# Second FFN: weights asked for behind a product's bank reads, a weight sum made with its own unit, the last down weights in the raw buffers

## The chip, the cores and the metric

The kernel runs on one core of a Trainium2 chip. The metric is the device time of one execution in microseconds. The time before is the median of three runs.

## What is computed

Two layers of a hybrid backbone over 512 latent and 256 context tokens, width 1024. Each layer is a mixer and then a gated FFN with a convolution over tokens; in the second layer only the latent tokens are needed. The change touches the second layer's FFN, with `z` of 512 x 1024, an up projection to 2 x 2816 and a down projection back to 1024:

```python
def conv_ffn(z, w_up, conv_w, conv_b, w_down):
    h = z @ w_up
    t = h.shape[1]
    half = CONV_W // 2
    hp = jnp.pad(h, ((0, 0), (half, half), (0, 0)))
    h = sum(hp[:, i:i + t] * conv_w[i] for i in range(CONV_W)) + conv_b
    a, g = jnp.split(h, 2, axis=-1)
    return (jax.nn.silu(g) * a) @ w_down
...
        hl = hl + mod_l[5] * conv_ffn(modulate(rms_norm(hl, norm2_g[layer]), mod_l[3], mod_l[4]),
                                      ffn_up[layer], ffn_conv_w[layer], ffn_conv_b[layer], ffn_down[layer])
...
    return rms_norm(hl, final_g)
```

## The kernel before

Each factor of a product is split into a high part (rounded to the matmul's type) and a low part (what is left), and one product is three matmuls: high by high, high by low, low by high. The FFN of the second layer is `layer1_end`; it runs from about 1216 us of the profile to the end.

**The up projection.** The 2816 features are 22 tiles of 128, p = 0 to 21. A tile stands for a gate tile and a value tile, so p has weights of 1024 x 256. For p = 0 and 1 it is made by plain block products ("C", `classical`). For p = 2 to 21 it is made by seven Strassen products ("S", `strassen`) over two halves of features and tokens. Each product is twelve matmuls of 128x256 (`product`, lines 1398 to 1400 in turn: high by high, high by low, low by high; the low half of the weights is read by line 1400 alone). P1, P6, P7 and P4 of one p accumulate into one PSUM bank, which ACT copies out after each (lines 1463, 1466, 1475, 1479); the next product into that bank waits for the copy. P5, P2 and P3 go to a second bank and are added by DVE (lines 1472, 1476, 1484). After P3(p), `finish(p)` makes the convolution (ACT line 1420 twice, DVE line 1422 four times), the Silu (ACT, line 1426), the product (DVE, line 1428) and the split into high and low (ACT line 131, DVE line 132). The order on TensorE, from one tile to the next, is P3(p-1), P6(p), P5(p), P2(p), P7(p), P1(p+1), P4(p), P3(p).

**The down projection** runs in eight chunks of features (3, 3, 3, 3, 3, 2, 2, 3 tiles). A step ("D") is three matmuls of 128x512; the steps of a chunk are woven between the products of later tiles, so that a D or two stand between most products. DVE adds a finished output tile to the stream (line 1498). The last chunk ("E") comes after the last product.

**Weight units.** `prepare` makes one unit: the factor of one product, or of one or two down steps. Its high half is a cast on ACT (line 1297). Its low half is either a subtraction on DVE (line 1303; A11, A12, S2 and down weights) or a negation on ACT (line 1300) and a DMA that POOL issues and that adds the source onto it (line 1301; S1, S3, S4, A22, and all of the first tiles). The product that takes the unit needs the DMA landed. S1 to S4 are sums of weight blocks, made on DVE (line 1318); all four are made when the tile's first unit, A11, is prepared. P1 takes A11, P2 A12, P3 S4, P4 A22, P5 S1, P6 S2 and P7 S3.

**What sets the order.** TensorE's order is written by hand in `events`. The other engines' instructions are ordered by the scheduler, which follows the order in which the code emits them and the waits it foresees. `weights(e)` asks for units up to five (`ASK`) ahead of the event's own in the order of use, and does so before the event's product is emitted. ACT, DVE and POOL each work in order, and so does SP, which issues the loads. Buffers are rings: 11 weight tiles (`WT`), 4 raw tiles of 1024 columns for up weights (`RAWS`), 2 raw tiles of 512 for down weights (`rawd`).

Of the kernel before, what the change touches and what calls it, by code (L numbers as in the profile page):

```python
# [10 lines left out]
F32 = mybir.dt.float32  # L11
F32R = mybir.dt.float32r
AF = mybir.ActivationFunctionType
ALU = mybir.AluOpType
# [22 lines left out]
PLAIN = 2  # L37
ASK = 5
# [3 lines left out]
def hybrid_backbone_kernel(ctx: ExitStack, tc: tile.TileContext, A: dict, out: bass.AP):  # L42
    nc = tc.nc
    pe, act, dve, pool = nc.tensor, nc.scalar, nc.vector, nc.gpsimd
# [3 lines left out]
    wp = ctx.enter_context(tc.tile_pool(name="wp", bufs=1))  # L48
# [3 lines left out]
    def nm(s):  # L52
        uid[0] += 1
        return f"{s}_{uid[0]}"

    def slab(dt=F32):
        return sb.tile([128, TW], dt, tag="slab", name=nm("sl"), bufs=SLAB)

    def half(dt=F32):
        return sb.tile([128, 512], dt, tag="half", name=nm("hf"), bufs=HALVES)  # L60
# [10 lines left out]
    def one():  # L71
        return pp.tile([128, 512], F32, tag="one", name=nm("on"), bufs=4)
# [4 lines left out]
    def bc(ap):  # L77
        return ap.bitcast(F32)
# [30 lines left out]
    def raw_tile(n):  # L109
        return wp.tile([128, n], F32, tag="raw", name=nm("raw"), bufs=RAWS, padded_shape=[128, 1024])  # L110

    def wtile(n=1024):
        return wp.tile([128, n], F32R, tag="w", name=nm("w"), bufs=WT, padded_shape=[128, 1024])
# [938 lines left out]
    for t in range(6):  # L1052
# [4 lines left out]
        if t < 4:  # L1057
            raw = half()
# [12 lines left out]
    for t in range(4):  # L1071
        raw = half()
# [169 lines left out]
    def layer1_end(x3, yds):  # L1242
# [8 lines left out]
        ch = CHUNKS[1]  # L1251
# [11 lines left out]
        for c in range(len(ch) - 1):  # L1263
# [3 lines left out]
            n = len(steps) - keep  # L1267
# [13 lines left out]
        def per(c):  # L1281
            return 2 if ch[c] <= 2 else 1

        def key(e):
            if e[0] == "C":
                return ("A", e[1], e[3])
            if e[0] == "S":
                return ("A", e[1], src_of[e[2]])
            return ("D", e[1], e[2] // per(e[1]))
# [3 lines left out]
        raws, sums, units = {}, {}, {}  # L1293
        asked = [0]

        def lows(h, l, src, by_dma):
            act.copy(out=h, in_=src)
            if by_dma:

                act.activation(out=l, in_=src, func=AF.Identity, scale=-1.0)  # L1300
                pool.dma_start(out=l, in_=src, accum_op=ALU.add)
            else:
                dve.tensor_tensor(out=l, in0=src, in1=bc(h), op=ALU.subtract)

        def prepare(k):
            if k[0] == "A":
                _, p, n = k
                if p not in raws:
                    rg, ra = raw_tile(1024), raw_tile(1024)
                    nc.sync.dma_start(out=rg, in_=A["ffn_up_w"][1, NF + p])  # L1310
                    nc.sync.dma_start(out=ra, in_=A["ffn_up_w"][1, p])
                    t = {"A11": rg[:, 0:512], "A12": rg[:, 512:1024], "A21": ra[:, 0:512], "A22": ra[:, 512:1024]}
                    raws[p] = t
                    if p >= PLAIN:
                        for o, x, y, op in (("S1", "A21", "A22", ALU.add), ("S2", "S1", "A11", ALU.subtract),
                                            ("S4", "A12", "S2", ALU.subtract), ("S3", "A11", "A21", ALU.subtract)):
                            t[o] = slab()[:, 0:512]
                            dve.tensor_tensor(out=t[o], in0=t[x], in1=t[y], op=op)
                w = wtile()
                h, l = w[:, 0:512], w[:, 512:1024]  # L1320
                lows(h, l, raws[p].pop(n), n in ("S1", "S3", "S4", "A22") or p < PLAIN + 2)
            else:
                _, c, u = k
                n, f0, w = per(c), ends[c] - ch[c], ch[c] * 128
                raw = wp.tile([128, 512], F32, tag="rawd", name=nm("rawd"), bufs=2)[:, :n * w]
                nc.sync.dma_start(out=raw.rearrange("p (m c) -> p m c", m=n),
                                  in_=A["ffn_down_w"][1, u * n:u * n + n, :, f0 * 128:f0 * 128 + w].rearrange(
                                      "m p c -> p m c"))
                t = wtile()
                h, l = t[:, 0:n * w], t[:, 512:512 + n * w]  # L1330
                lows(h, l, raw, False)
            return h, l

        def weights(e, ahead=ASK):
            i = seq.index(key(e))
            while asked[0] < min(len(seq), i + 1 + ahead):
                units[seq[asked[0]]] = prepare(seq[asked[0]])
                asked[0] += 1
            return units[seq[i]]
# [110 lines left out]

        def strassen(p, n):
            w = weights(("S", p, n))
            if n == "P1":
                zb[p] = one()[:, 0:256]
                hidden(p)
            if n == "P5":
                t = two()
                xy[p] = (t[:, 0:256], t[:, 512:768])
            hg, ha = hs[p]
            z = zb.get(p)  # L1460
            if n == "P1":
                product(z, w, B["B11"], True, False)
                act.copy(out=hg[:, H0], in_=z)  # L1463
            elif n == "P6":
                product(z, w, B["T2"], False, False)
                act.copy(out=hg[:, H1], in_=z)
            elif n == "P5":
                product(xy[p][0], w, B["T1"], True, False)
            elif n == "P2":
                y = xy[p][1]  # L1470
                product(y, w, B["B21"])
                dve.tensor_tensor(out=hg[:, H0], in0=y, in1=hg[:, H0], op=ALU.add)
            elif n == "P7":
                product(z, w, B["T3"], False, False)
                act.copy(out=ha[:, H1], in_=z)
                dve.tensor_tensor(out=ha[:, H1], in0=xy[p][0], in1=ha[:, H1], op=ALU.add)
            elif n == "P4":
                product(z, w, B["T4"], False, True)
                act.copy(out=ha[:, H0], in_=z)
                del zb[p]  # L1480
            else:
                x = xy.pop(p)[0]
                product(x, w, B["B22"], False, True)
                dve.tensor_tensor(out=hg[:, H1], in0=x, in1=hg[:, H1], op=ALU.add)
                finish(p)
# [3 lines left out]
        def down(e, a=0, b=512):  # L1489
            c, m, i = e[1:4]  # L1490
            h, l = weights(e)
            if i == 0:
                acc[0] = (two() if e[0] == "E" and a else one())[:, 0:b - a]
            o = (m % per(c)) * ch[c] * 128 + i * 128
            uh, ul = us[ends[c] - ch[c] + i]
            mm3(acc[0], (h[:, o:o + 128], l[:, o:o + 128]), (uh[:, a:b], ul[:, a:b]), i == 0, i == ch[c] - 1)
            if i == ch[c] - 1:
                dve.scalar_tensor_tensor(out=x3[:, m, a:b], in0=acc[0], scalar=modT[1][:, 0, 40 + m:41 + m],
                                         in1=x3[:, m, a:b], op0=ALU.mult, op1=ALU.add)
                if m == KT - 1 and (e[0] == "D" or a):  # L1500
                    for f in range(ends[c] - ch[c], ends[c]):
                        del us[f]
# [41 lines left out]
        with tc.manual_schedule(engines={mybir.EngineType.PE}):  # L1544
            for m in range(KT):
                part(0, m)
            for m in range(KT):
                part(1, m)
                if m == 2:
                    rows[0][1]()  # L1550
                if m == 4:
                    normed(0, rows[0][2]())
            yds.clear()
            for n, e in enumerate(events):
                if e[0] == "C":
                    classical(*e[1:])
                    if n == 0:
                        rows[1][1]()
                    if n == 2:
                        rb = rows[1][2]()  # L1560
                    if n == 4:
                        normed(1, rb)
                        differences()
                elif e[0] == "S":
                    strassen(*e[1:])
                elif e[0] == "D":
                    down(e)
                else:
                    _, _, m, i, gi = e
                    down(e, *GH[gi][:2])  # L1570
                    if i < ch[-1] - 1:
                        continue
                    final[gi][0]((m,))
                    if gi == 1 and m == 2:
                        final[0][1]()
                    if gi == 1 and m == 4:
                        normed_out(0)
            final[1][1]()
            normed_out(1)

    layer1_end(x3, yds)


# [111 lines left out]
```

## Time and profile before

| | |
|---|---|
| median of 3 runs | 1602.92 us (1601.92 to 1606.02) |
| the profiled execution: its time | 1602.01 us |
| the profiled execution: its span | 1600.2 us |
| TensorE busy | 1539.1 us, 96% of the span |
| DVE, ACT, POOL busy | 69%, 50%, 22% |
| chain of work that ended last | TensorE 86%, DVE 5%, ACT 3%, DMA 2% |

The span is what the profiler saw between the first and the last instruction; the 1.8 us around it belong to the execution's time. TensorE carries the chain. Idle time of the other engines costs nothing unless TensorE waits for them, so the table by stretches and TensorE's own waits are the views to read, and after them the timeline of the engine that each wait names.

### The profile page before, as it was taken

The page shows a single profiled execution, that of the slowest core. Times are in us where ns is not written, and L with a number is a line of the kernel's source. Part 1 is how long each engine was busy: PE and PEld are TensorE (multiplying, and loading weights), DVE is VectorE, ACT ScalarE, POOL GpSimd, SP SyncE. Part 2 cuts the span into 40 slices and gives each one's busy share as a digit, 9 for nine tenths or more (in the row PEclk, how much of TensorE's full clock was granted, in tenths as well). Part 3 has the DMA queues.
Part 4 walks back from the last instruction along what each step waited for, and adds up shares of the span by engine and source line. Part 5 has one row for each costly group of instructions (what it writes and reads, how often), then busy time and mean ns, then how long its engine had stood idle before and what let it go on. Part 6 is the DMA issues. An engine that isn't in the chain of part 4 may idle for free.

```text
span 1600.2 us, 25191 instructions
## 1 busy us (share of the span) xinstructions
PE 1539.1 (96%) x9394; PEld 1290.4 (81%) x9394; DVE 1106.6 (69%) x1955; ACT 806.1 (50%) x1574; POOL 353.0 (22%) x607
## 2 busy tenths in 40 slices
PE   6998999999999999999999999999999799999996
PEld 3786666658888888888888888778779799999986
DVE  4667765575469967865487557866667788877775
ACT  4447876674334233232331324535666767766663
POOL 0146444440011011010100100122324222222213
PEclk9999999999999999999999999999999899999998
DMA  9410014354123523622254211321134677776651
GB/s 314 158 53 27 1 53 159 106 172 164 54 80 112 158 66 122 208 65 66 66 172 145 63 57 45 108 66 40 40 87 99 146 181 172 165 175 161 167 119 65
DMA packets 81068, 179.19 MB, mean 112 GB/s; under 512 B 9393, under 2 KB 23729, under 8 KB 80945
## 3 DMA queue, kind: packets, MB, share of 16 engines
q1 hardware_dynamic: 67408, 152.93, 30.4%
q0 software_dynamic: 13536, 24.65, 9.0%
q8 instruction: 74, 1.21, 0.3%
q14 instruction: 50, 0.40, 0.1%
HBM read 150.80 MB, written 2.10 MB: 96 GB/s over the span
## 4 chain that ended last, share of the span: by engine, by line
PE 86%; DVE 5%; ACT 3%; issue 2%; DMA 2%; POOL 1%; SPq 0%; DVEq 0%; ACTq 0%; POOLq 0%
PE tw L125 9%; PE tw L126 9%; PE tw L127 9%; PE on L125 8%; PE on L126 7%; PE on L127 7%; PE on L621 3%; PE on L613 2%; PE on L1398 2%; PE on L1399 2%; PE on L1400 2%; PE tw L298 2%; PE tw L295 2%; PE tw L297 2%; PE tw L1398 2%
## 5 line engine op out<-in xcount | busy, mean ns | idle before, releaser
L125 PE MATMUL tw<-sl,w 128*128 128x512 f32 (+1 forms) x832 | 281.9, 339 | 0.1
L126 PE MATMUL tw<-sl,w 128*128 128x512 f32 (+1 forms) x832 | 280.9, 338 | 0.0
L127 PE MATMUL tw<-sl,w 128*128 128x512 f32 (+1 forms) x832 | 280.3, 337 | 0.0
L120 DVE TENSOR_TENSOR w<-raw,w 128x1024 fp32r<-128x1024 f32 (+3 forms) x119 | 137.7, 1159 | 139.8 <-PE tw L126 98.9
L119 ACT CAST w<-raw 128x1024 fp32r<-128x1024 f32 (+3 forms) x119 | 117.4, 990 | 175.3 <-PE tw L127 152.7
L125 PEld LDWEIGHTS tw<-sl,w 128*128 128x128 f32 x832 | 157.1, 189 | 27.4 <-issue 3.6
L125 PE MATMUL on<-sl,w 128*128 128x512 f32 (+2 forms) x504 | 174.0, 346 | 0.0
L126 PEld LDWEIGHTS tw<-sl,w 128*128 128x128 f32 x832 | 157.1, 189 | 18.9 <-issue 0.8
L127 PE MATMUL on<-sl,w 128*128 128x512 f32 (+2 forms) x504 | 171.7, 341 | 0.0
L126 PE MATMUL on<-sl,w 128*128 128x512 f32 (+2 forms) x504 | 171.7, 341 | 0.0
L127 PEld LDWEIGHTS tw<-sl,w 128*128 128x128 f32 x832 | 156.8, 188 | 17.7
L945 POOL TENSOR_SCALAR sm<-sm,csum,cw 128x2 f32<-128x2 f32 x44 | 30.3, 690 | 477.4 <-ACT sm L944 477.4
L1398 PE MATMUL on<-sl,w 128*128 128x256 f32 x384 | 109.8, 286 | 11.0 <-ACT sl L1463 9.9
L572 POOL TENSOR_SCALAR sl<-sl,sm 128x768 f32<-128x768 f32 (+2 forms) x96 | 84.7, 883 | 159.8 <-DVE sm L571 137.6
L125 PEld LDWEIGHTS on<-sl,w 128*128 128x128 f32 x504 | 95.6, 190 | 19.3 <-issue 7.3
L1399 PE MATMUL on<-sl,w 128*128 128x256 f32 x384 | 109.3, 285 | 0.0
L1400 PE MATMUL on<-sl,w 128*128 128x256 f32 x384 | 109.1, 284 | 0.0
L127 PEld LDWEIGHTS on<-sl,w 128*128 128x128 f32 x504 | 95.3, 189 | 11.1
L126 PEld LDWEIGHTS on<-sl,w 128*128 128x128 f32 x504 | 95.7, 190 | 9.8 <-DVE sl L132 0.2
L963 DVE SCALAR_TENSOR_TENSOR sl<-sl,cw,sl 128x770 f32<-128x770 f32 x88 | 89.4, 1019 | 19.6 <-ACT sl L960 17.9
L570 ACT ACTIVATE sl<-tw,sm 128x768 f32<-128x768 f32 (+2 forms) x96 | 81.8, 852 | 40.2 <-DVE sm L569 32.9
L569 DVE TENSOR_REDUCE sm<-tw 128x1 f32<-128x768 f32 (+2 forms) x96 | 84.9, 886 | 18.2 <-PE tw L787 12.0
(318 smaller groups left out, 3829.0 us busy)
## 6 DMA issues: line engine op xcount, KB each, us to landing
raw<-in_ffn_up_w_dram SPq DMA_DIRECT2D x88, 512.0 KB, 3.7
mraw<-in_mod_w_dram SPq DMA_DIRECT2D x96, 256.0 KB, 3.6
raw<-in_mod_w_dram SPq DMA_DIRECT2D x32, 512.0 KB, 4.0
w<-sl POOLq DMA_DIRECT2D x62, 256.0 KB, 4.1
rawd<-in_ffn_down_w_dram SPq DMA_DIRECT2D x48, 192.0 KB, 3.6
sl<-in_mod_w_dram SPq DMA_DIRECT2D x32, 256.0 KB, 5.4
raw<-in_ffn_down_w_dram SPq DMA_DIRECT2D x16, 512.0 KB, 3.6
w<-raw POOLq DMA_DIRECT2D x32, 256.0 KB, 4.4
```

The source lines that it names most:

```text
L119: act.copy(out=h, in_=raw)
L120: dve.tensor_tensor(out=l, in0=raw, in1=bc(h), op=ALU.subtract)
L125: pe.matmul(out=ps, lhsT=lh, rhs=rh, start=first, stop=False)
L126: pe.matmul(out=ps, lhsT=lh, rhs=rl, start=False, stop=False)
L127: pe.matmul(out=ps, lhsT=ll, rhs=rh, start=False, stop=last)
L569: dve.tensor_reduce(out=st[:, 0:1], in_=ps, axis=AX.X, op=ALU.max, negate=True)
L570: act.activation(out=p, in_=ps, func=AF.Exp, bias=st[:, 0:1], accum_out=st[:, 1:2])
L572: pool.tensor_scalar(out=p, in0=p, scalar1=st[:, 2:3], scalar2=1.0, op0=ALU.mult, op1=ALU.mult)
L963: dve.scalar_tensor_tensor(out=r[:, 2:end], in0=h[:, 2 + o:end + o], scalar=cw[:, f, t:t + 1], in1=r[:, 2:end], op0=ALU.mult, op1=ALU.add)
L1398: pe.matmul(out=ps, lhsT=h[:, o], rhs=rh, start=(first and k == 0), stop=False, skip_group_check=True)
L1399: pe.matmul(out=ps, lhsT=h[:, o], rhs=rl, start=False, stop=False, skip_group_check=True)
L1400: pe.matmul(out=ps, lhsT=l[:, o], rhs=rh, start=False, stop=(last and k == 3), skip_group_check=True)
```

## The change

Three edits in `layer1_end`:

1. `weights(e)` before a product or a down step asks for nothing ahead of the unit that it needs. The request for the five units ahead is made again, as `weights(e, ASK)`, after the product, its bank reads and, for P3, the `finish` have been emitted. (`classical` gives its own count ahead and keeps it.)
2. The four weight sums of a tile are no longer made at its first unit. Each is made in `part_of` when its own unit is prepared, S1 with S2. The raw tiles are held until the last of them, S4, is made.
3. The down weights of the last chunk are loaded into the ring of raw tiles (4 of them) instead of `rawd` (2).

TensorE's order is the same before and after.

```diff
+        def part_of(p, n):
+            t = raws[p]
+            if n not in t:
+                x, y, op = {"S1": ("A21", "A22", ALU.add), "S2": ("S1", "A11", ALU.subtract),
+                            "S4": ("A12", "S2", ALU.subtract), "S3": ("A11", "A21", ALU.subtract)}[n]
+                x, y = part_of(p, x), part_of(p, y)
+                t[n] = slab()[:, 0:512]
+                dve.tensor_tensor(out=t[n], in0=x, in1=y, op=op)
+            return t[n]
+
         def prepare(k):
             if k[0] == "A":
                 _, p, n = k
...
                     raws[p] = t
-                    if p >= PLAIN:
-                        for o, x, y, op in (("S1", "A21", "A22", ALU.add), ("S2", "S1", "A11", ALU.subtract),
-                                            ("S4", "A12", "S2", ALU.subtract), ("S3", "A11", "A21", ALU.subtract)):
-                            t[o] = slab()[:, 0:512]
-                            dve.tensor_tensor(out=t[o], in0=t[x], in1=t[y], op=op)
                 w = wtile()
                 h, l = w[:, 0:512], w[:, 512:1024]
-                lows(h, l, raws[p].pop(n), n in ("S1", "S3", "S4", "A22") or p < PLAIN + 2)
+                lows(h, l, part_of(p, n), n in ("S1", "S3", "S4", "A22") or p < PLAIN + 2)
             else:
                 _, c, u = k
                 n, f0, w = per(c), ends[c] - ch[c], ch[c] * 128
-                raw = wp.tile([128, 512], F32, tag="rawd", name=nm("rawd"), bufs=2)[:, :n * w]
+                if c < len(ch) - 1:
+                    raw = wp.tile([128, 512], F32, tag="rawd", name=nm("rawd"), bufs=2)[:, :n * w]
+                else:
+                    raw = raw_tile(n * w)
...
-        def weights(e, ahead=ASK):
+        def weights(e, ahead=0):
...
                 elif e[0] == "S":
                     strassen(*e[1:])
+                    weights(e, ASK)
                 elif e[0] == "D":
                     down(e)
+                    weights(e, ASK)
                 else:
                     _, _, m, i, gi = e
                     down(e, *GH[gi][:2])
+                    weights(e, ASK)
```

In the rows below, `w_...` is a weight tile, `sl_...` a working tile, `raw_...` a loaded up weight, `rawd_...` a loaded down weight, `on_...` a PSUM bank. In the changed kernel lines 1420, 1426, 1428, 1463, 1466, 1475 and 1479 have become 1428, 1434, 1436, 1471, 1474, 1483 and 1487; the sum's line 1318 is now 1312.

ACT around the copy of the first Strassen product, P1(2), before. The cast of `w_2271_12401` is that of a weight sum of p = 2:

```order
L1426 ACTIVATE sl_2252_12311<-sl_2252_12311 128x512
L131 ACTIVATE hf_2249_12256<-sl_2248_12251 128x512
L1297 CAST w_2271_12401<-sl_2261_12339 128x512
L1300 ACTIVATE w_2271_12401<-sl_2261_12339 128x512
L131 ACTIVATE hf_2254_12321<-sl_2253_12316 128x512
L1463 COPY sl_2266_12350<-on_2265_12349 128x256
```

ACT at the same place, after:

```order
L1428 ACTIVATE sl_2251_12312<-sl_2243_12186,cw_2126_11561 128x512
L1434 ACTIVATE sl_2250_12307<-sl_2250_12307 128x512
L131 ACTIVATE hf_2247_12252<-sl_2246_12247 128x512
L1471 COPY sl_2255_12322<-on_2254_12321 128x256
L1297 CAST w_2258_12343<-sl_2259_12344 128x512
L1300 ACTIVATE w_2258_12343<-sl_2259_12344 128x512
```

The copy (line 1463, now 1471) has moved ahead of the weight cast and of the second tile's high part; it stands directly behind the first tile's high part (line 131).

ACT from the cast of S3(6) to `finish(5)`, before. `w_2369_13064` is the unit S3(6), which P7(6) takes; `w_2381_13125` is A22(6) and `w_2382_13142` S4(6); lines 1475 and 1479 are the copies of P7(5) and P4(5), line 1463 that of P1(6):

```order
L1297 CAST w_2369_13064<-sl_2348_12911 128x512
L1475 COPY sl_2331_12800<-on_2329_12798 128x256
L1300 ACTIVATE w_2369_13064<-sl_2348_12911 128x512
L1297 CAST w_2377_13084<-raw_2371_13072 128x512
L1463 COPY sl_2360_12992<-on_2359_12991 128x256
L1297 CAST w_2379_13105<-rawd_2378_13103 128x384
L1479 COPY sl_2331_12800<-on_2329_12798 128x256
L1297 CAST w_2381_13125<-raw_2344_12902 128x512
L1300 ACTIVATE w_2381_13125<-raw_2344_12902 128x512
L1297 CAST w_2382_13142<-sl_2347_12909 128x512
L1300 ACTIVATE w_2382_13142<-sl_2347_12909 128x512
L1420 ACTIVATE sl_2365_13050<-sl_2330_12799,cw_2126_11561 128x512
```

ACT in `finish(5)`, after. `w_2368_13064` is S3(6):

```order
L1428 ACTIVATE sl_2361_13041<-sl_2327_12791,cw_2126_11561 128x512
L1428 ACTIVATE sl_2362_13046<-sl_2328_12792,cw_2126_11561 128x512
L1474 COPY sl_2357_12984<-on_2356_12983 128x256
L1434 ACTIVATE sl_2361_13041<-sl_2361_13041 128x512
L131 ACTIVATE sl_2363_13051<-sl_2362_13046 128x512
L1297 CAST w_2368_13064<-sl_2369_13065 128x512
L1300 ACTIVATE w_2368_13064<-sl_2369_13065 128x512
```

The cast of S3(6) stood ahead of P7(5)'s copy; now it stands behind the convolutions, the Silu and the high part of `finish(5)`, which comes after P4(5)'s copy.

DVE where the sum for S3(6), `sl_2348_12911`, is made, before; line 132 is the low part of `finish(4)`:

```order
L1472 TENSOR_TENSOR sl_2330_12799<-tw_2350_12916,sl_2330_12799 128x256
L132 TENSOR_TENSOR u_2340_12873<-sl_2338_12867,u_2339_12872 128x512
L1318 TENSOR_TENSOR sl_2347_12909<-raw_2343_12901,sl_2346_12907 128x512
L1318 TENSOR_TENSOR sl_2348_12911<-raw_2343_12901,raw_2344_12902 128x512
L1498 SCALAR_TENSOR_TENSOR big_964_4011<-on_2352_12933,modT1_95,big_964_4011 128x512
L1303 TENSOR_TENSOR w_2356_12980<-sl_2346_12907,w_2356_12980 128x512
```

DVE where that sum, `sl_2369_13065`, is made, after; lines 1430, 1436 and 132 belong to `finish(5)`:

```order
L1430 SCALAR_TENSOR_TENSOR sl_2361_13041<-sl_2327_12791,cw_2126_11561,sl_2361_13041 128x512
L1430 SCALAR_TENSOR_TENSOR sl_2362_13046<-sl_2328_12792,cw_2126_11561,sl_2362_13046 128x512
L1430 SCALAR_TENSOR_TENSOR sl_2361_13041<-sl_2327_12791,cw_2126_11561,sl_2361_13041 128x512
L1430 SCALAR_TENSOR_TENSOR sl_2362_13046<-sl_2328_12792,cw_2126_11561,sl_2362_13046 128x512
L1436 TENSOR_TENSOR sl_2362_13046<-sl_2361_13041,sl_2362_13046 128x512
L1506 SCALAR_TENSOR_TENSOR big_964_4011<-on_2367_13060,modT1_95,big_964_4011 128x512
L132 TENSOR_TENSOR sl_2364_13052<-sl_2362_13046,sl_2363_13051 128x512
L1312 TENSOR_TENSOR sl_2369_13065<-raw_2343_12912,raw_2344_12913 128x512
```

The sum has moved from behind `finish(4)` to behind `finish(5)`.

ACT from the copy of P7(9) to that of P4(9), before. `w_2486_13832` is S3(10), `w_2495_13868` A22(10):

```order
L1475 COPY sl_2448_13565<-on_2446_13563 128x256
L1297 CAST w_2486_13832<-sl_2463_13654 128x512
L1300 ACTIVATE w_2486_13832<-sl_2463_13654 128x512
L1297 CAST w_2493_13861<-raw_2487_13849 128x512
L1463 COPY sl_2475_13752<-on_2474_13751 128x256
L1297 CAST w_2495_13868<-raw_2459_13645 128x512
L1300 ACTIVATE w_2495_13868<-raw_2459_13645 128x512
L1479 COPY sl_2448_13565<-on_2446_13563 128x256
```

ACT in `finish(9)`, after. `w_2484_13841` is S3(10):

```order
L1428 ACTIVATE sl_2478_13805<-sl_2444_13556,cw_2126_11561 128x512
L1428 ACTIVATE sl_2479_13810<-sl_2445_13557,cw_2126_11561 128x512
L1474 COPY sl_2471_13743<-on_2470_13742 128x256
L1434 ACTIVATE sl_2478_13805<-sl_2478_13805 128x512
L1297 CAST w_2484_13841<-sl_2485_13842 128x512
L1300 ACTIVATE w_2484_13841<-sl_2485_13842 128x512
```

S3(10) stood ahead of P1(10)'s copy; now it stands behind the convolutions and the Silu of `finish(9)`.

## Rows read from the trace of the kernel before

**Rows 1.** Of the page: the engines' busy time:

```profile
PE 1539.1 (96%) x9394; PEld 1290.4 (81%) x9394; DVE 1106.6 (69%) x1955; ACT 806.1 (50%) x1574; POOL 353.0 (22%) x607
```

**Rows 2.** Busy time by engine in stretches of 50 us (columns in the first line):

```profile
core 0: us, PE busy (x) PEld busy (x) DVE busy (x) ACT busy (x) POOL busy (x), PEclk, DMA share, GB/s
...
1250.00:1300.00 50.00, 43.98 (x315) 41.76 (x316) 36.23 (x63) 35.65 (x71) 12.91 (x24) 0.91 0.72 165
1300.00:1350.00 50.00, 50.00 (x350) 46.65 (x349) 41.40 (x71) 34.89 (x69) 10.98 (x18) 1.00 0.73 173
```

**Rows 3.** Timeline of ACT, 1245 to 1256.5 us (columns: start, us, what, idle before):

```profile
1250.90 0.63 ACT L131 ACTIVATE hf<-sl 128x512 fp32r<-128x512 f32 x1
1253.97 0.62 ACT L1297 CAST w<-sl 128x512 fp32r<-128x512 f32 x1 [2.44 <-DVE sl L1318]
...
1255.03 0.61 ACT L131 ACTIVATE hf<-sl 128x512 fp32r<-128x512 f32 x1
1255.55 0.35 ACT L1463 COPY sl<-on 128x256 f32<-128x256 f32 x1
```

**Rows 4.** Timeline of PE, 1245.9 to 1256.3 us:

```profile
1255.95 0.58 PE L1398 MATMUL on<-sl,w 128*128 128x256 f32 x1 [9.89 <-ACT sl L1463]
```

**Rows 5.** Timeline of ACT, 1545.5 to 1552.5 us:

```profile
1548.90 0.51 ACT L1297 CAST w<-rawd 128x384 fp32r<-128x384 f32 x1 [0.99 <-DMA rawd<-in_ffn_down_w_dram]
...
1549.85 0.35 ACT L1475 COPY sl<-on 128x256 f32<-128x256 f32 x1
```

**Rows 6.** Timeline of PE, 1547.2 to 1551.6 us, and the stretch behind it by engine:

```profile
1547.58 0.28 PE L1400 MATMUL on<-sl,w 128*128 128x256 f32 x1
1551.06 0.38 PE L1398 MATMUL tw<-sl,w 128*128 128x256 f32 x1 [3.20 <-DVE sl L1476]
...
1552.50:1555.90 3.40, 3.40 (x13) 2.82 (x12) 1.33 (x3) 0.51 (x1) 0.00 (x0) 0.50 0.39 115
```

**Rows 7.** Timeline of DVE, 1358 to 1367 us: the end of feature tile 8:

```profile
1360.14 2.79 DVE L1422 SCALAR_TENSOR_TENSOR sl<-sl,cw,sl 128x512 f32<-128x512 f32 x4 [0.44 <-ACT sl L1420]
1362.84 0.69 DVE L1318 TENSOR_TENSOR sl<-sl,raw 128x512 f32<-128x512 f32 x1
1363.44 0.69 DVE L1428 TENSOR_TENSOR sl<-sl,sl 128x512 f32<-128x512 f32 x1
...
1365.25 0.68 DVE L132 TENSOR_TENSOR u<-sl,hf 128x512 fp32r<-128x512 f32 x1
...
1366.51 0.41 DVE L1472 TENSOR_TENSOR sl<-tw,sl 128x256 f32<-128x256 f32 x1
```

**Rows 8.** Timeline of ACT, 1357.5 to 1377 us:

```profile
1362.30 0.63 ACT L1426 ACTIVATE sl<-sl 128x512 f32<-128x512 f32 x1 [1.14 <-DVE sl L1422]
...
1364.50 0.63 ACT L131 ACTIVATE hf<-sl 128x512 fp32r<-128x512 f32 x1
...
1368.08 0.62 ACT L1297 CAST w<-sl 128x512 fp32r<-128x512 f32 x1
1368.60 0.63 ACT L1300 ACTIVATE w<-sl 128x512 fp32r<-128x512 f32 x1
...
1370.76 0.63 ACT L1300 ACTIVATE w<-raw 128x512 fp32r<-128x512 f32 x1
```

**Rows 9.** Timelines of PE, last matmul of P3(8), first of P7(9), P3(9), P7(10):

```profile
1358.35 0.28 PE L1400 MATMUL tw<-sl,w 128*128 128x256 f32 x1
...
1366.19 0.28 PE L1398 MATMUL on<-sl,w 128*128 128x256 f32 x1
...
1372.53 0.28 PE L1398 MATMUL tw<-sl,w 128*128 128x256 f32 x1
...
1381.68 0.28 PE L1398 MATMUL on<-sl,w 128*128 128x256 f32 x1
```

**Rows 10.** Timeline of POOL, 1351 to 1376 us:

```profile
1371.68 0.86 POOL L1301 DMA_DIRECT2D w<-raw  x1 [1.15 <-ACT w L1300]
```

**Rows 11.** Line 1301, the accumulating DMAs, 1216 to 1545 us: issue to landing:

```profile
DMA to landing us min/median/max: 3.2/4.3/7.1
```

## The prediction

> **What bounds the kernel now.** I read the page's busy shares first: TensorE is busy 1539.1 us of the span [rows 1], so the change can only matter where TensorE waits, or where it comes to wait. The change touches the second FFN alone, which runs from about 1216 us to the end. There the table of 50-us stretches comes next: 43.98 of 50 us busy in 1250 to 1300, then 50.00 in 1300 to 1350, and the same in the two stretches behind it; DVE is busy 41.40 and ACT 34.89 of 50 in that stretch [rows 2]. So in the middle of the FFN nothing is to be gained at all, and the question is whether the work around TensorE keeps its lead. There are two waits of size. In the first, TensorE stands 9.89 us until 1255.95 for the copy of P1(2)'s bank on ACT, line 1463 [rows 4]; ACT's timeline shows why: the copy begins at 1255.55, right behind a weight cast that itself waited 2.44 us for a weight sum on DVE, and behind the second hi part of `finish` [rows 3]. In the last, TensorE stands 3.20 us until 1551.06 for DVE's line 1476 [rows 6]; that reads what ACT copied in line 1475, at 1549.85, and ahead of the copy on ACT stands a cast that had waited 0.99 us for a down-weight load [rows 5]. Behind that wait TensorE runs 3.40 us at a granted clock of 0.50, the lower level [rows 6].
>
> **Part 1, what is gained.** Requests that come behind a product's bank reads put the reads first on ACT. For P1(2) the order of the changed kernel has the copy directly behind the first hi part of `finish`, with no cast ahead of it. That hi part starts at 1250.90, and the next instruction on ACT starts 0.52 behind such a one (1255.03 to 1255.55), so the copy starts at 1251.42 instead of 1255.55: 4.1 us gained [rows 3]. At the end, the last chunk's down weights lie in the ring of four raw buffers instead of two, and are asked behind the bank reads. P7(21) ends at 1547.58 + 0.28 = 1547.86 [rows 6], so the copy could start 1.95 us earlier than 1549.85 [rows 5]; the half-clock stretch of 3.40 us, which costs half of itself, 1.7, goes too. What is late next is the accumulating DMA of S1(21), which now starts later as well; I put 0.9 on it (between 0 and the 3.20 that stands there now): 2.7 gained. Together 6.8. An upper end for this part is the whole 9.89 instead of 4.1, if the `finish` ahead of the copy cost nothing: 5.8 more.
>
> **Part 2, what is lost.** The same edit moves the requests of S3(p), A22(p) and S4(p) behind the `finish(p-1)` that follows P3(p-1), and the second edit moves their sums on DVE there too. Nothing is added (the number of sums, casts and DMAs is the same; DVE has as much work), so all of the price is lateness. How much lead there was: S3(10) was cast at 1368.08 [rows 8] and first used by P7(10) at 1381.68 [rows 9], 13.6 us later. Now its cast stands on ACT behind the two conv activations and the Silu of `finish(9)`, and ACT works in order, so it can't start before them. I count from E, the end of P3(p-1), and take the times from tile 8, where E = 1358.35 + 0.28 = 1358.63; P7(9) starts at 1366.19 = E+7.56 and P3(9) at 1372.53 = E+13.90 [rows 9]. The low half of a weight is read first by a product's third matmul, 0.24 later (two 128x256 matmuls): at E+7.80 and E+14.14.
>
> Three patterns stand in the changed order. Pattern b (p = 4, 7, 10, 13, 19): the sum for S3 stands on DVE behind the four conv sums of line 1422. The next DVE instruction behind those starts at 1362.84 = E+4.21 and takes 0.69 [rows 7]: E+4.90. Then the cast, 0.52 to the low part and 0.63 for that [rows 8]: E+6.05. POOL issues the accumulating DMA 0.29 later (ACT's low part ends at 1370.76 + 0.63 = 1371.39, the DMA starts at 1371.68) [rows 8, 10]: E+6.34. It lands 3.2, 4.3 or 7.1 us later (least, median, most) [rows 11]: with the median at E+10.64, against E+7.80. TensorE waits 2.8 us at P7(p). For p = 19 a down step of 0.7 is missing ahead of P7, so 3.5.
>
> Pattern c (p = 6, 12, 18): the sum stands on DVE behind the product of line 1428, a chunk's addition and the lo part, and the cast behind the hi part. Silu ends at 1362.30 + 0.63 = E+4.30 [rows 8]; the product takes 0.69, hi 0.63 and lo 0.68 one after the other, with 0.05 between: sum at about E+6.4, done at E+7.1; cast, low part and issue as above, 1.44 more: E+8.54; landed at E+12.84. TensorE waits 5.0 us [rows 7, 8].
>
> Pattern a (p = 5, 8, 9, 11, 14): S3 comes in time there, but S4(p) stands behind P2's addition, line 1472, which starts at 1366.51 = E+7.88 [rows 7]. Its sum ends near E+8.9, the DMA starts near E+10.35 and lands at E+14.65, against E+14.14: 0.5 us each. At p = 15 to 17 and 20 more down steps lie between, and I count nothing. For p = 2 and 3, whose units all take the DMA, I count one wait of pattern b and a quarter of another, 3.5 together.
>
> Sum of the waits: 4 x 2.8 + 3.5 + 3 x 5.0 + 5 x 0.5 + 3.5 = 35.7. The clock: a wait of 3.20 was followed by a half-clock stretch that cost 1.7 [rows 6], and pattern c's waits are longer, so 3 x 1.7 = 5.1; pattern b's are shorter, and I count nothing in the sum and 1.7 each in the upper end.
>
> How long the DMA takes decides most of this. The Trainium skill (DMA: Bandwidth & Descriptors, section Anatomy of one DMA, SWDGE path) gives a fixed 2 us or so plus the bytes at 436 GB/s, an estimate of 2.6 us for these 256 KB; with that the waits would be 1.1, 3.3 and 0, and the sum of both parts about 11, a time near 1613, on the side of the first rival below, which is worked out without it. The trace disagrees: none of these DMAs landed in under 3.2 us [rows 11].
>
> Other queues: POOL's memsets for the next tile's banks are moved along with the DMAs, ahead of the next product's copy; S4's later sum frees the raw buffers later, so SP's next up-weight load is issued behind it, yet that load serves the tile after the next and has a whole period of 15 us in hand (1366.19 to 1381.68, [rows 9]). Both are hidden.
>
> **Sum.** The profiled execution took 1602.01 us, the median of the runs is 1602.92. 35.7 + 5.1 - 6.8 = +34.0: 1636.0 against the profiled execution, 1637 against the median.
>
> **Rivals.**
> Less is lost: the DMAs land in their least time, 3.2, since raw loads no longer fall on them, and no clock is lost. Then pattern b costs 1.7, c 3.9, a nothing, p = 19 2.4, the first two 2.1: 6.8 + 2.4 + 11.7 + 2.1 = 23.0, less 6.8: +16, 1619. For it: the stalls themselves thin the DMA traffic. Against it: 3.2 is the least of 86.
> More is lost: the DMAs fall on raw and down loads and take 5.3, and pattern b's waits cost the clock too. 15 waits by 1.0 and 5 x 1.7 more: +57.5, 1660. For it: the most was 7.1 [rows 11].
> Faster, the other side: the two waits go and no unit comes late. It decides at the cast of S3(p): were it on ACT ahead of `finish(p-1)`'s conv activations, as it is now at 1368.08 against use at 1381.68, the gains alone would stay: 1602.92 - 6.8 = 1596. Against it stands the order itself, in which S3 is behind the Silu in patterns b and c, and the in-order rows of ACT.
> No change: gains and losses cancel. That needs waits at P7 of under 1 us, thus DMAs under 2.5 us, which no row shows: 1603.
>
> **How the numbers follow.** Forecast 1637: 0.60. Less is lost, 1619: 0.17. More is lost, 1660: 0.13. Faster, 1596: 0.06. No change: 0.04. The measurement tells about 0.3% from no change, 4.8 us. So slower 0.90, same 0.04, faster 0.06. The range goes from 1613 (the lesser loss with the upper end of part 1) to 1660, and leaves out some 0.15.
>
> **What would show it.** In the profile after: the wait on line 1463's copy (now 1471) shrinks from 9.89 to some 5.8; the stretches from 1300 to 1450 no longer show 50.00 busy; TensorE waits on line 1408 for DMA `w<-sl`, at P7(6), P7(12) and P7(18) by some 5 us, at P7(4, 7, 10, 13, 19) by some 3; half-clock stretches behind the longest. The prediction is wrong if those rows are missing, or if they are there and DMAs land in 3.2 us or less.

## The result: 1665 us, slower by more than was forecast

The changed kernel takes 1664.96 us (median of 4 runs, 1660.9 to 1671.6) against 1602.42 before: a ratio of 1.0397, interval 1.0368 to 1.0427. Slower was forecast, at 1637 with a range up to 1660; the loss is 62 us where 34 were predicted. The span of the profiled execution went from 1600.2 to 1662.3, 62.1 more.

TensorE's waits in the profile after, from 1240 us to the end (who waited for whom, us in total, times, longest):

```profile
PE on L1408 <- DMA w<-sl: 32.9, 9, 5.3
PE tw L1408 <- DMA w<-sl: 14.8, 9, 3.8
PE on L1406 <- ACT sl L1471: 5.4, 1, 5.4
...
PE tw L1406 <- DVE sl L1484: 0.9, 1, 0.9
```

The first wait, for P1(2)'s copy, is 5.4 us where 9.89 stood [rows 4]. New are 47.7 us of waits on a product's third matmul, for an accumulating DMA: 32.9 into the `on` bank, which is P7 and so S3, and 14.8 into `tw`, which is P3 and so S4 but for 1.3 at P5(21), which takes S1. The wait near the end, 3.20 before [rows 6], is 0.9. The table by stretches shows them where TensorE had no idle time (columns as in [rows 2]):

```profile
1300.00:1350.00 50.00, 45.04 (x294) 41.44 (x294) 33.21 (x56) 27.76 (x56) 8.08 (x13) 0.93 0.54 127
1350.00:1400.00 50.00, 44.04 (x292) 40.38 (x291) 33.34 (x58) 29.82 (x61) 10.81 (x18) 0.97 0.68 158
1400.00:1450.00 50.00, 40.02 (x261) 36.27 (x260) 34.83 (x59) 29.56 (x58) 9.92 (x17) 0.95 0.54 127
```

Against 50.00 of 50 us busy at a clock of 1.00 [rows 2], TensorE is busy 40 to 45 us, and the granted clock is 0.93 to 0.97.

The sum over the whole FFN: gaps between the starts of neighbouring matmuls, over what such a matmul takes and over 0.25 us, come to 23.3 us in 1200 to the end before and 69.1 after, 45.8 more. TensorE's busy time at the lower clock, from 1240 on, is 7.7 us before and 41.4 after; counted as half lost, as in the prediction, the 33.7 more cost 16.9. Together 62.7, against 62.1 in the span. (Half is a little much: matmuls of 128x256 start 0.213 us apart at a clock of 0.50 and 0.118 apart at 1.00 in this profile, which makes it 45%, or 15.)

### The profile page after: what moved, and what is told of

Its sections match the earlier page's. It is cut to its first block, busy times and chain, and to the rows that moved or that the text cites. A ratio compares the mean times of both kernels' runs of the same rounds, so it can differ in the third digit from the quotient of the medians.

```text
span 1662.3 us, 25186 instructions
## 1 busy us (share of the span) xinstructions
PE 1559.6 (94%) x9394; PEld 1305.6 (79%) x9394; DVE 1108.6 (67%) x1955; ACT 805.7 (48%) x1574; POOL 354.1 (21%) x607
## 4 chain that ended last, share of the span: by engine, by line
PE 76%; DMA 8%; DVE 6%; ACT 4%; issue 4%; POOL 1%; SPq 0%; DVEq 0%; POOLq 0%; ACTq 0%
PE tw L125 9%; PE tw L126 9%; PE tw L127 9%; PE on L125 6%; PE on L126 6%; PE on L127 6%; DMA w<-sl 6%; PE on L621 3%; PE on L613 2%; PE tw L295 2%; PE tw L298 2%; PE tw L297 2%; PE on L1408 2%; PE on L154 1%; PE on L1406 1%
## 5 line engine op out<-in xcount | busy, mean ns | idle before, releaser
L1408 PE MATMUL on<-sl,w 128*128 128x256 f32 x384 | 115.8, 302 | 32.9 <-DMA w<-sl 32.9
L1406 PE MATMUL on<-sl,w 128*128 128x256 f32 x384 | 115.3, 300 | 6.7 <-ACT sl L1471 5.4
L1407 PE MATMUL on<-sl,w 128*128 128x256 f32 x384 | 114.0, 297 | 0.0
L1301 POOL DMA_DIRECT2D w<-sl x62 | 53.6, 865 | 268.8 <-ACT sl L1474 68.3
L125 PEld LDWEIGHTS on<-sl,w 128*128 128x128 f32 x504 | 95.3, 189 | 19.5 <-issue 7.4
L1408 PEld LDWEIGHTS on<-sl,w 128*128 128x128 f32 x384 | 79.3, 206 | 35.1 <-DMA w<-sl 35.0
L127 PEld LDWEIGHTS on<-sl,w 128*128 128x128 f32 x504 | 95.2, 189 | 11.1
L126 PEld LDWEIGHTS on<-sl,w 128*128 128x128 f32 x504 | 95.4, 189 | 9.7 <-DVE sl L132 0.2
```

The lines of the kernel that those rows point to most:

```text
L125: pe.matmul(out=ps, lhsT=lh, rhs=rh, start=first, stop=False)
L126: pe.matmul(out=ps, lhsT=lh, rhs=rl, start=False, stop=False)
L127: pe.matmul(out=ps, lhsT=ll, rhs=rh, start=False, stop=last)
L1406: pe.matmul(out=ps, lhsT=h[:, o], rhs=rh, start=(first and k == 0), stop=False, skip_group_check=True)
L1407: pe.matmul(out=ps, lhsT=h[:, o], rhs=rl, start=False, stop=False, skip_group_check=True)
L1408: pe.matmul(out=ps, lhsT=l[:, o], rhs=rh, start=False, stop=(last and k == 3), skip_group_check=True)
```

## One late weight, followed through the engines

Pattern c at P7(6). DVE, ACT, POOL and TensorE in turn (start, duration, what, idle before and who ended it):

```profile
1321.62 2.79 DVE L1430 SCALAR_TENSOR_TENSOR sl<-sl,cw,sl 128x512 f32<-128x512 f32 x4 [1.03 <-ACT sl L1428]
1324.51 0.69 DVE L1436 TENSOR_TENSOR sl<-sl,sl 128x512 f32<-128x512 f32 x1
...
1325.90 0.69 DVE L132 TENSOR_TENSOR sl<-sl,sl 128x512 fp32r<-128x512 f32 x1
1326.51 0.68 DVE L1312 TENSOR_TENSOR sl<-raw,raw 128x512 f32<-128x512 f32 x1
```

```profile
1327.23 0.62 ACT L1297 CAST w<-sl 128x512 fp32r<-128x512 f32 x1 [1.36 <-DVE sl L1312]
1327.75 0.63 ACT L1300 ACTIVATE w<-sl 128x512 fp32r<-128x512 f32 x1
```

```profile
1328.82 0.87 POOL L1301 DMA_DIRECT2D w<-sl  x1 [10.83 <-DVE sl L1312]
```

```profile
1328.12 0.28 PE L1407 MATMUL on<-sl,w 128*128 128x256 f32 x1
1333.29 0.58 PE L1408 MATMUL on<-sl,w 128*128 128x256 f32 x1 [4.89 <-DMA w<-sl]
```

The four conv sums, the product and the low part of `finish(5)` run on DVE, and only then the sum for S3(6), 1326.51. ACT had waited 1.36 us for it. Behind the low part (1327.75 + 0.63) the DMA starts 0.44 later, lands 4.4 us later, and TensorE stands 4.89 us between P7(6)'s second and third matmul. The prediction had 5.0 for this.

A late S4 is another matter. P3(16): POOL and SP at the start of its accumulating DMA, that DMA's own time, and TensorE at the end:

```profile
1526.88 0.86 POOL L1301 DMA_DIRECT2D w<-sl  x1 [3.90 <-ACT sl L1483]
```

```profile
1526.11 0.33 SPq L1320 DMA_DIRECT2D raw<-in_ffn_up_w_dram  x1
1526.54 0.38 SPq L1334 DMA_DIRECT2D rawd<-in_ffn_down_w_dram  x1
1526.97 0.46 SPq L1321 DMA_DIRECT2D raw<-in_ffn_up_w_dram  x1
```

```profile
DMA to landing us min/median/max: 7.8/7.8/7.8
```

```profile
1534.76 0.39 PE L1408 MATMUL tw<-sl,w 128*128 128x256 f32 x1 [1.87 <-DMA w<-sl]
```

Both up-weight loads of a later tile, 512 KB each, and a down load start within 0.9 us of the DMA, which lands 7.8 us after its start. The two loads go into the two raw tiles of this p. S4's sum is the last reader of the one, and A22's accumulating DMA, issued shortly before, of the other. SP's own waits, first around P3(8), then at P3(16), show both:

```profile
SPq L1320 <- DVE sl L1312: 3.2, 1, 3.2
SPq L1321 <- DMA w<-raw: 0.7, 1, 0.7
```

```profile
SPq L1320 <- DMA w<-raw: 3.8, 1, 3.8
```

## Experiments

**The three edits one by one.** The first alone (`e_behind`):

```diff
-        def weights(e, ahead=ASK):
+        def weights(e, ahead=0):
...
                     strassen(*e[1:])
+                    weights(e, ASK)
...
                     down(e)
+                    weights(e, ASK)
```

> The first edit alone: requests behind the bank reads, all four sums still made at a tile's first unit, last down weights in the small ring. Theory 1 (the sums made with their own units are what comes late): no wait on the third matmul line of a product in 1300 to 1450, the first wait (9.9 us on P1(2)'s copy) shorter by about 4, time about 1598, from 1595 to 1602. Theory 2 (the requests behind the bank reads and behind finish are what comes late): the 5-us and 3-us waits at P7 stay, time 1645 to 1665.

Measured 1599.35 us, ratio 0.9982 (0.9972 to 0.9992). TensorE's waits there:

```profile
PE on L1398 <- ACT sl L1463: 5.8, 1, 5.8
PE tw L1398 <- DVE sl L1476: 2.8, 1, 2.8
```

The first wait shrank by 4.1 and no DMA is waited for. So theory 2 falls: requests behind the bank reads, with the sums made early, gain a little and cost nothing.

The second alone (`e_sums`: `part_of` as in the change, `ahead=ASK` as before, `rawd` for all chunks):

> The second edit alone: each sum made when its own unit is prepared, requests ahead as before, last down weights in the small ring. Theory 1: the waits of the changed kernel at P7 of tiles 4, 6, 7, 10, 12, 13 and so on stay, 3 and 5 us each, about 25 us together, and half-clock stretches behind them cost another 10 to 15; time 1635 to 1650. Theory 2: no such waits, time within 4 us of 1602.

Measured 1636.08 us, ratio 1.0225 (1.0203 to 1.0247): 34 slower, as theory 1 has it. TensorE's waits from 1240 us to the end:

```profile
PE on L1405 <- DMA w<-sl: 25.0, 7, 5.5
PE tw L1405 <- DMA w<-sl: 6.4, 4, 2.4
PE on L1403 <- ACT sl L1468: 5.4, 1, 5.4
```

The waits at P7 and P3 are there, 25.0 and 5.3 us (the other 1.1 of the 6.4 is at P5(21)), with requests made as early as before. The sum is what is late. The first edit then adds to it: with both, the code asks for each unit one step later still, and the loss goes from 34 to 62. The first wait, for P1(2)'s copy, is 5.4 us here too: the second edit by itself shortens it as much as the first does, so that this gain does not add up over the two.

The third alone (`e_raw`):

```diff
+                if c < len(ch) - 1:
+                    raw = wp.tile([128, 512], F32, tag="rawd", name=nm("rawd"), bufs=2)[:, :n * w]
+                else:
+                    raw = raw_tile(n * w)
```

> The third edit alone: the last chunk's down weights in the ring of four raw buffers. Both theories: nothing changes before 1500; the wait of 3.2 us near 1551 gets 1 us shorter or more, and its half-clock stretch may go; time 1598 to 1601.

Measured 1601.77 us, ratio 1.0006 (0.9992 to 1.0020): no change that can be told. The wait at the end is still there:

```profile
PE tw L1401 <- DVE sl L1479: 3.0, 1, 3.0
```

3.0 us against 3.20 [rows 6], so the ring of two alone was not what held the copy of P7(21).

The first and third together (`e_behind_raw`):

> The first and third edits together, without the second. Theory 1: both gains and none of the loss, about 6 to 7 us faster than before: 1596, from 1593 to 1600. Theory 2: as slow as the first edit alone, 1645 to 1665.

Measured 1597.5 us, ratio 0.9982 (0.9969 to 0.9995). Neither loss nor more than the first edit's gain.

**Is it the landing of the DMA?** The changed kernel, low parts of S3 and S4 by a subtraction on DVE (`t_lowdve`):

```diff
-                lows(h, l, part_of(p, n), n in ("S1", "S3", "S4", "A22") or p < PLAIN + 2)
+                lows(h, l, part_of(p, n), n in ("S1", "A22") or p < PLAIN + 2)
```

> The changed kernel, with the low parts of S3 and S4 subtracted on DVE instead of by ACT and an accumulating DMA. Theory 1 (the landing of a DMA that is issued late is what TensorE waits for): the waits for DMA w<-sl at P7 fall from 3 to 5 us to under 1.6 and those at P3 to about 0.7, waits in all some 25 to 30 us shorter, the half-clock stretches in 1290 to 1600 go; time 1612 to 1625. Theory 3 (ACT and DVE are simply too late or too loaded in the new order, DMA or not): time above 1645.

Measured 1612.67 us, ratio 1.0059 (1.0038 to 1.0079): 52 of the 62 us are gone. At P7(6) the cast is as late as in the changed kernel, where ACT waited the same 1.36 us for the sum, and TensorE waits 0.38 us instead of 4.89:

```profile
1321.88 0.62 ACT L1297 CAST w<-sl 128x512 fp32r<-128x512 f32 x1 [1.36 <-DVE sl L1312]
```

```profile
1323.44 0.39 PE L1408 MATMUL on<-sl,w 128*128 128x256 f32 x1 [0.38 <-DVE w L1303]
```

So what TensorE waited for was the DMA behind the late cast, not the engines. The waits that are left are mostly for the DMAs that this run keeps, 10.4 us in all.

S4 alone on DVE (`t_s4dve`):

> The changed kernel with the low part of S4 alone subtracted on DVE instead of by a DMA. S3 stays with its DMA. If S4's share of the loss is its DMA, the waits at P3 (14.6 us of waits on the third matmul line into the tw bank) go nearly all, and those at P7 stay near 35; time 1645 to 1655. If P3 waits for the sum or the cast, they stay.

Measured 1652.66 us in one run. TensorE's waits from 1240 us to the end:

```profile
PE on L1408 <- DMA w<-sl: 34.6, 9, 5.3
...
PE tw L1408 <- DMA w<-sl: 4.6, 2, 3.5
```

The waits into `tw` fall from 14.8 to 4.6: 3.5 in an early tile whose units all take the DMA, and 1.1 at P5(21). Those into `on`, at P7, stay: 34.6 against 32.9. So of the 52 us that S3's and S4's DMAs are worth together, S4's is worth some 12; that leaves about 40 for S3's, which was not run alone.

**Is it the lead?** The changed kernel with `ASK = 7` (`t_ask7`):

> The changed kernel with ASK = 7 instead of 5, so that a unit and its sum are asked for two units earlier. Theory 1 (only the lead is lost): the casts of S3 stand ahead of finish again, no wait for DMA w<-sl over 1 us, time 1595 to 1602. Theory 3 (the sums made one by one cost by themselves, on DVE or in held raw buffers): time above 1620.

Measured 1598.92 us, ratio 0.9975 (0.9964 to 0.9986). All three edits stand in this kernel and the loss is gone:

```profile
PE on L1406 <- ACT sl L1471: 5.4, 1, 5.4
PE tw L1406 <- DVE sl L1484: 3.1, 1, 3.1
PE on L1408 <- DMA w<-sl: 1.6, 2, 1.1
```

1.6 us of waits for the DMA, of 47.7. A sum made with its own unit costs nothing once the unit is asked for early enough. Theory 3 falls.

**What one wait costs with the clock.** The kernel before, one sum late (`t_two`):

```diff
+LATE = (6, 12, 18)
...
+                            if o == "S3" and p in LATE:
+                                continue
...
+                if n == "S3" and p in LATE:
+                    raws[p][n] = slab()[:, 0:512]
+                    dve.tensor_tensor(out=raws[p][n], in0=raws[p]["A11_"], in1=raws[p]["A21"], op=ALU.subtract)
```

> The kernel before, with one thing alone made late: the sum for S3 of tiles 6, 12 and 18 is made when its unit is prepared, all else as before. By the orders that puts two waits of about 4.6 us at P7(6) and P7(12), some 100 us apart, and none at P7(18). Theory A (a wait costs itself and a half-clock stretch of 6.8 us behind it): 2 x (4.6 + 3.4) = 16 slower, 1618. Theory B (a stretch of 3.4 us behind it, as the prediction took it): 2 x (4.6 + 1.7) = 13 slower, 1615. Theory C (the clock costs nothing here): 9 slower, 1611.

Measured 1615.87 us, ratio 1.0083 (1.0063 to 1.0104), that is 13.3 us (10 to 17) for two waits; the span is 13.8 longer. The waits, and the stretches behind them with busy time by engine, clock in the third last column:

```profile
PE on L1407 <- DMA w<-sl: 7.8, 2, 4.0
```

```profile
1323.20:1329.90 6.70, 6.21 (x26) 5.92 (x27) 3.31 (x6) 2.78 (x7) 1.54 (x2) 0.50 0.87 215
1422.20:1428.90 6.70, 5.09 (x21) 4.80 (x22) 2.93 (x7) 4.03 (x9) 2.59 (x3) 0.50 0.91 167
```

Each wait of 4 us comes with 6.8 us at the lower clock, of which TensorE is busy 6.2 and 5.1: half of that, 2.8 on the mean, is lost. So a wait of 4.0 costs 6.8. The span agrees (2 x 6.8 = 13.6, against 13.8). The stretch is as long as theory A has it; the waits are shorter than the 4.6 expected and TensorE is not busy all through the stretch, so the sum comes out between A's 16 and B's 13. By the time alone the interval leaves both standing and drops theory C's 9.

**Why S4's DMA takes so long.** The changed kernel with `RAWS = 5` and `SLAB = 31` (`t_raws5`):

> The changed kernel with 5 raw buffers instead of 4 (and 31 working slabs instead of 33, for the room). Disputed: why S4's accumulating DMAs take 5.6 to 7.8 us in the changed kernel where S3's take 4.3 to 5.1. If it is the two up-weight loads that S4's own sum sets free and that start with it, one of the two now goes earlier: S4's DMAs land in 4.3 to 5.5 us and the waits at P3 shrink from 1.4 to 2.2 to about 1; the waits at P7 of 3 and 5 us stay. If it is something else (the place of S4 in the POOL queue, down loads), S4's DMAs stay at 5.6 and more.

1662.38 us in one run. This did not tell the two apart, since the edit didn't move the loads:

```profile
1369.89 0.33 SPq L1321 DMA_DIRECT2D raw<-in_ffn_up_w_dram  x1
1371.05 0.33 SPq L1320 DMA_DIRECT2D raw<-in_ffn_up_w_dram  x1
```

```profile
1371.34 0.86 POOL L1301 DMA_DIRECT2D w<-sl  x1 [2.81 <-ACT sl L1483]
```

Both up loads still start within 1.5 us of S4's DMA, which took 6.9. So the loads themselves were taken away, in the changed kernel (`t_noload`):

```diff
-                    rg, ra = raw_tile(1024), raw_tile(1024)
-                    nc.sync.dma_start(out=rg, in_=A["ffn_up_w"][1, NF + p])
-                    nc.sync.dma_start(out=ra, in_=A["ffn_up_w"][1, p])
+                    if p < 4:
+                        kept[0] = raw_tile(1024), raw_tile(1024)
+                        nc.sync.dma_start(out=kept[0][0], in_=A["ffn_up_w"][1, NF + p])
+                        nc.sync.dma_start(out=kept[0][1], in_=A["ffn_up_w"][1, p])
+                    rg, ra = kept[0]
```

> The changed kernel without the up-weight loads of tiles 4 to 21: these tiles read the raw weights of tile 3 again, so the output is another, and casts, sums, accumulating DMAs and their order stay. Disputed: why S4's DMAs take 5.6 to 7.8 us. If the 512 KB up loads in flight with them are the cause, S4's DMAs land in 3.3 to 4.5 us, S3's in 3.2 to 4.3 instead of 4.3 to 5.1; the waits at P3 (14.8 us) fall under 3, those at P7 (32.9) to about 25, and with fewer half-clock stretches the time is 1630 to 1645. If S4's DMAs stay at 5.5 us and more, the cause is elsewhere.

Measured 1626.76 us in one run, 38 less than the changed kernel. Its waits, and the time to landing of its accumulating DMAs in 1320 to 1530:

```profile
PE on L1411 <- DMA w<-sl: 21.8, 8, 4.6
...
PE tw L1411 <- DMA w<-sl: 1.3, 1, 1.3
```

```profile
DMA to landing us min/median/max: 3.2/3.6/5.5
```

S4(16)'s DMA, which took 7.8 in the changed kernel:

```profile
DMA to landing us min/median/max: 3.3/3.3/3.3
```

The median is 3.6 us, against 4.5 in the changed kernel in about the same stretch (most 7.8). The one wait left in `tw`, 1.3 us, is at P5(21) and not for S4: the waits for S4 are gone, and those at P7 have fallen from 32.9 to 21.8. The sums, the casts, their order and the down loads are still there, so the up loads in flight were what made S4's DMA slow, and a part of S3's.

**A version that gains.** First the first and third edits with `ASK = 6` (`t_ask6`):

> The first and third edits without the second, and ASK = 6. By theory 1 no unit is late; the wait for P1(2)'s copy is 6 us, the one at the end about 2: 1594 to 1598, at best 2 us under the same kernel with ASK = 5.

1596.75 us, ratio 0.9968 (0.9953 to 0.9982). Then, in addition, the `finish` of the two classical tiles held back behind P1(2) (`t_held`):

```diff
                 if i == 1:
-                    finish(p)
+                    held.append(p)
...
                     strassen(*e[1:])
+                    while held:
+                        finish(held.pop(0))
```

> A version from what was found: first and third edits, ASK = 6, and the two finish calls of the classical tiles held back until P1(2) and its copy have been emitted. The wait of 6 us for that copy should fall to about 1, with waits of 1.6 us each at P5(2) or P2(2) and P7(2) new; no unit late behind that; no half-clock stretch of 6.8 us at 1250. Time 1590 to 1595, some 3 to 5 us under the same kernel without the held calls.

Measured 1592.05 us, ratio 0.9932 (0.9917 to 0.9948): about 11 us faster than before (8 to 13), and some 73 under the changed kernel. TensorE at P1(2)'s copy:

```profile
1249.58 0.39 PE L1402 MATMUL on<-sl,w 128*128 128x256 f32 x1 [0.83 <-ACT sl L1467]
```

0.83 us where 9.89 stood [rows 4].

## Why the prediction came out as it did

**Right.** The direction, the place and the mechanism: S3's cast behind `finish`, TensorE waiting at the third matmul of P7 for the DMA. Pattern c was put at 5.0 and the three are 4.9 to 5.3 (over the normal matmul spacing). Pattern b was put at 2.8 and is 2.6, 3.6, 3.3 and 3.3. The first wait was to shrink to some 5.8 and is 5.4, though not by the first edit only: either edit alone brings that, 5.8 in `e_behind` and 5.4 in `e_sums`.

**Wrong, first: how long S4's DMA takes.** The sum took the median of 4.3 for every DMA, and the paragraph on other queues called SP's later up-weight load hidden. It has time enough for its own reader, but both loads of the pair start about when S4's DMA does: S4's DMAs that were waited for in tiles 8 to 17 took 5.6 to 7.8 us. Pattern a, put at 0.5 for five tiles and at nothing for 15 to 17, is 1.4 to 2.2 at tiles 8, 9, 11, 14, 16 and 17 and 0.7 at 15, 10.8 in all against 2.5 (tile 5 waited not at all). P7(19) is 5.5 against 3.5 with a DMA of 6.2, and the first two tiles are 6.0 against 3.5. All waits: 45.8 more than before, against 35.7 less 5.1 predicted. `t_noload` shows the cause: with no up load in flight, the waits of pattern a are gone.

**Wrong, second: the clock.** The sum had 1.7 each behind pattern c, 5.1, less 1.7 at the end. The profile after gives 16.9, with the same half. Behind the longest waits of that profile the lower clock stands for 6.8 us and not for 3.4, and four waits of 3.3 to 4.0 us are followed by 3.4 us of it, which the sum left to the upper end:

```profile
1332.60:1339.30 6.70, 6.01 (x25) 5.72 (x26) 2.64 (x6) 2.05 (x5) 0.86 (x1) 0.50 1.00 235
1356.50:1359.80 3.30, 3.30 (x15) 3.01 (x14) 1.68 (x3) 2.34 (x5) 0.71 (x1) 0.50 0.84 213
1411.10:1414.40 3.30, 3.30 (x14) 3.01 (x14) 1.68 (x3) 2.35 (x5) 0.86 (x1) 0.50 0.88 217
1297.00:1300.40 3.40, 3.40 (x27) 3.22 (x26) 1.12 (x2) 2.25 (x6) 0.01 (x1) 1.00 0.82 187
```

These are the stretches behind P7(6), P7(7), P7(10) and P7(4), whose waits are 5.0, 3.6, 3.3 and 2.6 (over the normal matmul spacing); behind the last the clock stayed. `t_two` prices a 4-us wait with its clock at 6.8. The two terms miss 15.2 and 13.5 us, which is the whole of the 28 us by which the loss was too small (12 for the second where 45% and not half is counted).

**Wrong, third: which edit.** The prediction gave the lateness to the first edit, with the second beside it. `e_behind` gains and `e_sums` loses 34: the second is what makes a unit late, and the first only deepens it. The 2.7 us for the end of the FFN was put on the third edit's larger ring; `e_raw` shows that it does nothing there. The wait does fall to 0.9 in the changed kernel, but with 1.3 new at P5(21) for S1's DMA, and it is back at 3.1 in `t_ask7`, with all three edits: it shrank because TensorE came later, not because the copy came sooner (argued from these runs, not tested by itself).

**The upper rival** ("more is lost", 1660, 0.13) had both mechanisms, the DMAs falling on loads and the clock at pattern b, and still a too small time for the DMA (5.3) and the clock (1.7).

## What to carry to other kernels

Work moved to "just before it is needed" has to be priced with what it releases: the sum that came last also freed a load buffer, just when the transfer ahead of it freed the other, and both loads started on top of the one transfer that TensorE waited for. Take the duration of a transfer from rows in which the same neighbours are in flight, not from the median of the line. And when a step loses its lead, ask for it further ahead before giving up the edit: two units more made all of the loss go.

## What was not expected of the hardware

The price of a wait did not follow from its length alone. In `t_noload`, with no up load in flight, two waits of 1.75 us at P7, until 1342.32 and 1447.28, were followed by different clocks (third last column):

```profile
1343.60:1347.00 3.40, 3.40 (x16) 3.12 (x15) 1.68 (x3) 2.34 (x5) 0.86 (x1) 0.51 0.77 160
1448.50:1451.90 3.40, 3.40 (x25) 3.14 (x25) 1.82 (x4) 3.08 (x7) 0.84 (x1) 1.00 0.81 169
```

Waits of 2.48 in the changed kernel and 2.41 in `e_sums` left the clock alone; waits of 2.51 in `t_raws5` and 2.58 in `t_held` did not. The waits of 3.2 to 3.5 us in the changed kernel and `e_sums` were followed by 3.4 us at the lower clock in six cases and by 6.8 us in one. Of the 20 waits of 3.8 to 5.5 us in the changed kernel, `e_sums`, `t_two`, `t_s4dve`, `t_raws5` and `t_noload` (those for P1(2)'s copy left out), 12 were followed by 6.8 us and 8 by 3.4 us. What decides isn't settled here. So a wait can cost nothing beyond itself, or the 1.7 of a 3.4-us stretch, or up to 3 us more than itself, and a sum of waits should carry a range for it.

The accumulating DMA of 256 KB landed in 3.2 to 5.5 us, 3.6 in the median, with no up load in flight, and in up to 7.8 with two up loads and a down load.
